# Batched matmul, 32 batches on one core: transposes of the last batches moved into their own batch, and one store split between two DMA issuers

## The chip, the cores and the metric

One core of one Trainium2 chip runs the program. The metric is device microseconds (us) of that core. The time that a run reports is about 1.7 to 2.0 us more than the span in its profile. In the profile PE is TensorE, DVE is VectorE, ACT is ScalarE, POOL is GpSimd and SP is SyncE.

## The reference

```python
def setup_inputs():
    batch, m, k, n = 32, 512, 1024, 768
    return {"x": np.random.randn(batch, m, k).astype(np.float32),
            "weight": np.random.randn(batch, k, n).astype(np.float32)}

def reference(x, weight):
    return np.matmul(x, weight).astype(np.float32)
```

Per batch the kernel reads 2 MB of x and 3 MB of weight, and writes 1.5 MB. All of it together is 168 MB read and 50 MB written.

## The kernel before

A batch's x and weight are loaded by POOL, which casts them to bf16 on the way. PE transposes x, multiplies, and ACT and DVE bring the sums from PSUM, the memory that PE writes to, to `out_sb`. The store of a batch goes out on POOL's queue one batch later. Only the first load and the two halves of the last store are issued by SP.

```python
out_view = out.rearrange("b (mi mo) n -> b mi (mo n)", mi=P)   # 12,288 bytes per partition
CHUNKED = {B - 4: (4, 4), B - 3: (4, 4), B - 2: (4, 4), B - 1: (4, 2, 2)}
AHEAD = 3
...
def load_x(b):
    xs[b] = x_pool.tile([P, MT, K], BF16, name="x_sb")
    nc.gpsimd.dma_start(out=xs[b], in_=x_view[b])
...
for b in range(B):
    if b + AHEAD < B:
        load_x(b + AHEAD)
        load_w(b + AHEAD)
    if b > 0:
        nc.gpsimd.dma_start(out=out_view[b - 1], in_=outs[b - 1])
    outs[b] = out_pool.tile([P, MT * N], F32, name="out_sb")
    if b not in CHUNKED:
        ...                                   # 28 batches, untouched by the change
        continue
    xT = ready.pop(b, None) or {mt: transpose(b, mt) for mt in range(MT)}
    pms = [banks() for _ in range(2)]
    at = 0
    for n in CHUNKED[b]:
        last = at + n == KT
        for mt in range(MT):
            if last and b + 1 < B:
                ready.setdefault(b + 1, {})[mt] = transpose(b + 1, mt)
            matmuls(pms[mt // 2], mt % 2, xT[mt], b, range(at, at + n), True)
            if last and mt % 2 == 1:
                pair = mt // 2
                evacuate(b, pair, pms[pair])
                if b == B - 1:
                    cols = slice(pair * N2, (pair + 1) * N2)
                    nc.sync.dma_start(out_view[b, :, cols], outs[b][:, cols])
        at += n
```

In the last four batches the weight comes in chunks, and the transposes of batch b+1 stand between the matmuls of batch b's last chunk. That holds for batches 29 to 31; batch 28, the first of the four, has its own transposes at its start.

## Time and profile before

| what | value |
|---|---|
| time, median of 6 runs | 516.88 us (516.58 to 517.77) |
| profiled run | 517.73 us, span 516.0 us |
| PE busy | 426.4 us (83%) |
| HBM traffic over the span | 423 GB/s |

From the page of the kernel before, the DMA rows of the 40 slices, and of the chain that ended last the first line:

```profile
DMA  8999999999999999999999999999999999999996
GB/s 255 218 218 211 215 274 275 272 272 241 255 280 273 275 254 241 276 277 274 267 240 268 274 276 272 247 252 278 275 274 256 247 267 275 276 267 239 259 390 261
...
DMA 88%; PE 9%; issue 1%; DVE 0%; ACT 0%; POOLq 0%
```

A 9 means that the sixteen DMA engines were busy for 90% of the slice or more. They are full everywhere but at the two ends, and the chain of waits is mostly transfers. So DMA bounds this kernel. Loads count at their bf16 size in this GB/s row (135.65 MB in all, where HBM saw 168 and 50 MB), so the row rises where only stores are left.

The table of stretches for the kernel before. Its columns are window, length, busy time (and count) of PE, PEld, DVE, ACT and POOL, the granted clock, the share of DMA (from packet times, so it can come out a little over 1) and GB/s:

```profile
41.00:440.00 399.00, 338.91 (x2011) 221.80 (x2049) 101.28 (x154) 60.26 (x103) 40.34 (x76) 0.94 1.02 263
490.00:505.00 15.00, 14.89 (x85) 9.49 (x86) 4.00 (x6) 2.35 (x4) 0.53 (x1) 0.89 1.03 392
505.00:516.00 11.00, 3.54 (x22) 1.95 (x20) 1.38 (x2) 2.30 (x4) 0.00 (x0) 0.90 0.56 231
```

DMA is saturated up to 505 us. Only after that is there slack, and PE is not what fills it.

The end of the timeline of the kernel before (start, length, engine, line, operation, count, and what ended the idle time before it):

```profile
489.12 0.75 PE L68 MATMUL pt<-ident,x_sb 128*128 128x128 f32 x4 [3.28 <-DMA x_sb<-in_x_dram]
...
496.67 11.86 PE L99 MATMUL pm<-w_sb,xT 128*128 128x256 bf16 x71
...
499.19 0.53 POOL L130 DMA_DIRECT2D out_dram<-out_sb  x1 [16.95 <-ACT out_sb L112]
...
507.89 1.62 SPq L159 DMA_DIRECT2D out_dram<-out_sb  x2
```

PE cannot finish batch 30 before x of batch 31 is there (489.12 us), so the store of batch 30 is issued at 499.19 us and the last two at 507.89 us and later.

The DMA queue's waits on SP, of the kernel before (who waited for whom, us in total, times, longest):

```profile
SPq L159 <- DVE out_sb L111: 507.5, 2, 506.7
SPq L186 <- DMA out_dram<-out_sb: 5.0, 3, 1.8
SPq L186 <- PEq L186: 0.9, 2, 0.5
```

L186 is the end of the program. SP waits there for the last transfers, and then for the other engines, for 0.9 us in two waits.

The trace also records when each of a transfer's sixteen completions arrived, one for each DMA engine that took part, without the engine's number. Sorted, they show how far the engines have drifted apart. These are the kernel before's, read from the completion records:

| transfer | first | last | spread |
|---|---|---|---|
| w, second load on POOL (batch 1) | 27.02 | 27.98 | 0.95 |
| x, landing at 199 us | 199.07 | 202.37 | 3.30 |
| store of batch 29 (POOL) | 502.26 | 507.45 | 5.19 |
| store of batch 30 (POOL) | 505.91 | 511.11 | 5.20 |
| batch 31, first half (SP) | 511.00 | 512.97 | 1.96 |
| batch 31, second half (SP) | 512.89 | 514.80 | 1.91 |

The engine that lands last is called the straggler below. It is 5 us behind the quickest at the end.

### The profile page before, as it was taken

What the parts mean: (1) busy time and instruction counts of PE and PEld (TensorE: products, weight loads), DVE (VectorE), ACT (ScalarE), POOL (GpSimd) and SP (SyncE); (2) the same over time, 40 slices, a digit from 0 to 9 for tenths busy, and PEclk for the clock granted to TensorE, in tenths of its full rate; (3) what the DMA queues carried; (4) which work ended last, traced back from release to release, by engine and by line L of the source; (5) the groups of instructions that cost most, each with busy time, mean ns of one, the idle gap of its engine ahead of it and who ended that gap; (6) DMA issues with size and microseconds to landing.
All of it is one profiled execution on the core that took longest, in us unless ns stands there. A gap on an engine that the chain in (4) does not pass through costs nothing.

```text
span 516.0 us, 5924 instructions
## 1 busy us (share of the span) xinstructions
PE 426.4 (83%) x2528; PEld 279.6 (54%) x2576; DVE 129.7 (25%) x196; ACT 76.3 (15%) x129; POOL 53.4 (10%) x105
## 2 busy tenths in 40 slices
PE   0999998698887879977798797987878987969794
PEld 0766665465554555654555464654545554646462
DVE  0433333133131231322313232222223132312221
ACT  0111111011111111110111011111111110101111
POOL 3011010100101001100011001010100110111000
PEclk9999999799898997998989799898989898979989
DMA  8999999999999999999999999999999999999996
GB/s 255 218 218 211 215 274 275 272 272 241 255 280 273 275 254 241 276 277 274 267 240 268 274 276 272 247 252 278 275 274 256 247 267 275 276 267 239 259 390 261
DMA packets 14714, 135.65 MB, mean 263 GB/s; under 512 B 1632, under 2 KB 1632, under 8 KB 3040
## 3 DMA queue, kind: packets, MB, share of 16 engines
q0 software_dynamic: 14256, 131.60, 98.9%
q1 hardware_dynamic: 432, 3.67, 1.9%
q8 instruction: 20, 0.33, 0.2%
q14 instruction: 6, 0.05, 0.0%
HBM read 167.77 MB, written 50.33 MB: 423 GB/s over the span
## 4 chain that ended last, share of the span: by engine, by line
DMA 88%; PE 9%; issue 1%; DVE 0%; ACT 0%; POOLq 0%
DMA x_sb<-in_x_dram 37%; DMA w_sb<-in_weight_dram 25%; DMA out_dram<-out_sb 24%; PE pm L99 7%; DMA x_first<-in_x_dram 2%; PE pt L81 1%; PE pt L68 1%; DVE out_sb L111 0%; DVE xT L70 0%; ACT out_sb L112 0%; POOLq L130 0%; POOLq L54 0%; POOLq L60 0%
## 5 line engine op out<-in xcount | busy, mean ns | idle before, releaser
L99 PE MATMUL pm<-w_sb,xT 128*128 128x256 bf16 (+1 forms) x2000 | 370.2, 340 | 60.9 <-DMA w_sb<-in_weight_dram 56.8
L99 PEld LDWEIGHTS <-xT 128*128 128x128 bf16 x2048 | 206.8, 102 | 198.3 <-issue 66.5
L70 DVE COPY xT<-pt 128x1024 bf16<-128x1024 bf16 x124 | 83.0, 689 | 245.4 <-PE pt L68 245.4
L68 PE MATMUL pt<-ident,x_sb 128*128 128x128 f32 x496 | 77.4, 290 | 8.9 <-DMA x_sb<-in_x_dram 8.6
L68 PEld LDWEIGHTS pt<-ident,x_sb 128*128 128x128 f32 x496 | 73.7, 207 | 17.2 <-issue 7.1
L110 ACT COPY out_sb<-pm 128x512 f32<-128x512 f32 x64 | 37.5, 586 | 289.6 <-PE pm L99 280.7
L111 DVE COPY out_sb<-pm 128x512 f32<-128x512 f32 x64 | 43.9, 687 | 115.5 <-PE pm L99 114.8
L112 ACT COPY out_sb<-pm 128x512 f32<-128x512 f32 x64 | 37.5, 586 | 142.5 <-PE pm L99 142.4
L54 POOL DMA_DIRECT2D x_sb<-in_x_dram x31 | 16.5, 533 | 172.8 <-DMA w_sb<-in_weight_dram 141.6
L60 POOL DMA_DIRECT2D w_sb<-in_weight_dram x37 | 19.8, 534 | 132.4 <-DMA out_dram<-out_sb 65.6
L130 POOL DMA_DIRECT2D out_dram<-out_sb x31 | 16.6, 536 | 140.8 <-DMA x_sb<-in_x_dram 62.8
L81 PE MATMUL pt<-ident,x_first 128*128 128x128 f32 x32 | 5.7, 338 | 12.4 <-DMA x_first<-in_x_dram 12.4
L81 PEld LDWEIGHTS pt<-ident,x_first 128*128 128x128 f32 x32 | 4.9, 202 | 13.0 <-issue 12.3
L82 DVE CAST xT<-pt 128x512 bf16<-128x512 f32 x8 | 5.5, 727 | 18.4 <-PE pt L81 18.3
L110 ACT ACT_TABLE_LOAD x1 | 1.3, 1283 | 0.7 <-PEq L175 0.7
masks.py:199 POOL TENSOR_SCALAR_AFFINE_SELECT ident<-ident 128x128 f32<-128x128 f32 x1 | 0.3, 288 | 0.1
masks.py:197 POOL MEMSET ident<- 128x128 f32 x1 | 0.2, 223 | 0.0
L175 POOL MEMSET const-float32-0.0<- 128x1 f32 x1 | 0.1, 99 | 0.2 <-issue 0.2
L175 POOL MEMSET const-bfloat16-1.0<- 128x1 bf16 x1 | 0.1, 102 | 0.0
L175 POOL MEMSET const-uint8-127<- 128x1 uint8 x1 | 0.1, 102 | 0.0
L175 POOL MEMSET const-float32-1.0<- 128x1 f32 x1 | 0.1, 98 | 0.0
## 6 DMA issues: line engine op xcount, KB each, us to landing
out_dram<-out_sb POOLq DMA_DIRECT2D x31, 1536.0 KB, 41.9
w_sb<-in_weight_dram POOLq DMA_DIRECT2D x28, 1536.0 KB, 43.2
x_sb<-in_x_dram POOLq DMA_DIRECT2D x31, 1024.0 KB, 39.6
w_sb<-in_weight_dram POOLq DMA_DIRECT2D x7, 768.0 KB, 32.5
x_first<-in_x_dram SPq DMA_DIRECT2D x1, 2048.0 KB, 11.5
out_dram<-out_sb SPq DMA_DIRECT2D x2, 768.0 KB, 5.3
w_sb<-in_weight_dram POOLq DMA_DIRECT2D x2, 384.0 KB, 28.7
```

What stands on the lines that cost most here:

```text
L54: nc.gpsimd.dma_start(out=xs[b], in_=x_view[b])
L60: nc.gpsimd.dma_start(out=ws[b][:, at:at + n, :], in_=w_view[b, :, at:at + n, :])
L68: nc.tensor.transpose(pt[:, j, :], pairs[:, mt, j::JT], ident)
L70: nc.vector.tensor_copy(xT.rearrange("p j m r -> p (j m r)"), pt.bitcast(BF16).rearrange("p j m -> p (j m)"))
L81: nc.tensor.transpose(pt[:, i, :], x_first[:, mt, JT * h + i::KT], ident)
L82: nc.vector.tensor_copy(xT[:, 2 * h:2 * h + 2].rearrange("p j m r -> p j r m"), pt.rearrange("p (j r) m -> p j r m", r=2),)
L99: nc.tensor.matmul(pm[bank][:, at:at + size], xT[:, ko // 2, :, ko % 2], ws[b][:, ko, off:off + size], start=(ko == 0 and not (together an ...
L110: nc.scalar.copy(o[:, 0:512], pm[0])
L111: nc.vector.tensor_copy(o[:, 512:1024], pm[1])
L112: nc.scalar.copy(o[:, 1024:N2], pm[2])
L130: nc.gpsimd.dma_start(out=out_view[b - 1], in_=outs[b - 1])
L175: nc = _bacc.Bacc("TRN2", target_bir_lowering=False, num_devices=1)
```

## The change

The change does two things. The transposes of the last four batches stand between their own matmuls (those of batches 29 to 31 come from the batch before), so PE need not hold the end of one batch until the next batch's x has landed. And the store of batch 8 is split: its first 32 partitions go as four eight-partition transfers on SP, and the other 96 as one on POOL. The likely intent of the second is to move a little load between the sixteen DMA engines.

```diff
+    FEW = {8}
...
+    def store(b):
+
+        first = 0
+        if b in FEW:
+            first = 32
+            for at in range(4):
+                nc.sync.dma_start(out_view[b, at:first:4], outs[b][at:first:4])
+        nc.gpsimd.dma_start(out=out_view[b, first:], in_=outs[b][first:])
...
-        ready = {}
...
-                nc.gpsimd.dma_start(out=out_view[b - 1], in_=outs[b - 1])
+                store(b - 1)
...
-            xT = ready.pop(b, None) or {mt: transpose(b, mt) for mt in range(MT)}
+            xT = {0: transpose(b, 0)}
...
-                    if last and b + 1 < B:
-                        ready.setdefault(b + 1, {})[mt] = transpose(b + 1, mt)
+                    if mt + 1 not in xT and mt + 1 < MT:
+                        xT[mt + 1] = transpose(b, mt + 1)
```

## The prediction

> **What bounds the kernel now.** The DMA engines. The page's DMA row is full in 39 of 40 slices; the chain of waits is 88% DMA; PE is busy 426 of 516 us. In the stretch table DMA is saturated from 2 to 505 us and falls to 0.56 after that. The trace's DMA completion records say why. Each transfer counts sixteen completions, one per engine, and these drift apart: spread 0.95 us at first, 3.3 us near 200 us, 5.2 us for the last POOL store (505.91 to 511.11 us). The steps coincide with the 20 instruction-fetch packets (16 KB, about 0.95 us each); their durations repeat with period eight, so they visit eight engines in rotation. After one rotation, at 199 us, seven engines lie within 0.6 us and nine trail by 1.2 to 3.3 us. The Trainium skill ("Runtime: NRT & Kernel Launch", Instruction fetch mechanics) describes refills in 16 KiB blocks; this trace agrees.
>
> The straggler is never idle: after 511.11 us it moves its 16 packets of the last two SP stores (0.235 us each, 3.7 us), landing at 514.80 us; the span ends 1.2 us later. Its total work is the time.
>
> **What the change does.**
>
> 1. Transposes. None is removed; twelve groups of four move from the previous batch's last chunk into their own batch. Today PE holds the last chunk of batch 30 until x of batch 31 lands (timeline: 489.12), runs to 508.5, and the store of batch 30 is issued at 499.19. Afterwards that store should be issued about 12 us earlier, PE end near 505 (estimate: w lands at 492.7, 64 matmuls at 168 ns, transposes), the last stores issue 4 us earlier. On the critical path: about nothing, since the straggler's queue is full anyway.
>
> 2. Store of batch 8. It moves 12,288-byte packets, eight per engine, each 0.457 us when stores run alone. By the skill ("DMA: Bandwidth & Descriptors", Why a DMA increments its semaphore by 16 and not by 1) an eight-partition SP transfer uses the lowest-numbered eight engines, and 96 partitions use all sixteen. So engines 0 to 7 carry 4+6=10 packets, 8 to 15 carry 6: plus or minus 0.91 us. No trace here numbers the engines; that the fetching, slow ones are 8 to 15 is a guess from the intent. If so, the straggler goes from 511.1 to 510.2, the fast half from at most 507.6 to 508.5: gain 0.9 us. If it is in 0 to 7, loss 0.9 us. Four more SP issues (0.34 us each) are off the path.
>
> **Predicted time: 516.1 us**, range 515.1 to 517.9 (8 in 10). Faster by over 2%: 0.01; within 2%: 0.98; slower by over 2%: 0.01. The 0.9 us gain has about 2 chances in 3.
>
> **What would show each step.**
> - Store: the last POOL store's completions: spread 5.2 to about 3.4 us; about 7 if the direction was wrong. Issue table: four 96 KB SP transfers, one 1152 KB POOL store.
> - Transposes: store of batch 30 issued before 490; PE's last matmul near 505; last SP stores near 504; yet the final landing unmoved by this.
> - Fetches: about 20, over eight engines.
>
> **What would make it wrong.** Fetching engines in both halves (gain then 0.2 or less); an altered fetch count or rotation; other engines for the eight-partition transfers; run-to-run spread (1.2 us, as large as the effect); or PE's tail mattering more than the straggler, worth up to 2 us more.

## The result, and the profile after

The changed kernel took 519.92 us (median of 6 runs, 519.24 to 520.54) against 516.88 us before. The ratio is 1.0056, with a 95% interval of 1.0043 to 1.0069. The change made the kernel slower by about 3 us. The predicted range ended at 517.9 us.

One caution for reading the two profiles against each other: the profiled run of before was its own slow end (517.73 us), and that of after was a little below its median (519.51 us). The two traces therefore differ by 1.8 us, not by 3.

The page of the changed kernel, the same rows:

```profile
DMA  8999999999999999999999999999999999999995
GB/s 254 218 216 212 225 263 278 272 276 244 252 292 272 276 250 230 272 276 274 270 246 256 276 275 273 261 240 273 277 274 269 243 261 271 277 270 258 238 410 216
...
DMA 81%; PE 14%; issue 1%; DVE 1%; ACT 0%; POOLq 0%
```

The table of stretches of the changed kernel:

```profile
41.00:440.00 399.00, 342.74 (x2061) 223.09 (x2059) 101.92 (x155) 60.29 (x103) 40.30 (x76) 0.94 1.02 263
490.00:505.00 15.00, 12.52 (x73) 7.91 (x72) 2.86 (x5) 0.61 (x2) 0.49 (x1) 0.89 1.03 391
505.00:516.00 11.00, 1.23 (x8) 0.58 (x6) 1.19 (x2) 1.68 (x3) 0.00 (x0) 0.73 0.56 236
```

DMA does the same work in the same stretches. PE, ACT and DVE have less left to do after 505 us, as intended.

The end of its timeline:

```profile
489.56 1.20 PE L69 MATMUL pt<-ident,x_sb 128*128 128x128 f32 x8 [0.66 <-DMA x_sb<-in_x_dram]
489.96 0.53 POOL L122 DMA_DIRECT2D out_dram<-out_sb  x1 [7.92 <-ACT out_sb L113]
...
498.27 7.96 PE L100 MATMUL pm<-w_sb,xT 128*128 128x512 bf16 x48
505.58 2.07 SPq L168 DMA_DIRECT2D out_dram<-out_sb  x2
```

The store of batch 30 is issued 9.2 us earlier and the last two 2.3 us earlier. The first part of the change did what it was meant to do.

The DMA queue's waits on SP, of the changed kernel:

```profile
SPq L168 <- DVE out_sb L112: 361.6, 2, 360.8
SPq L121 <- DVE out_sb L112: 140.5, 1, 140.5
SPq L195 <- DMA out_dram<-out_sb: 7.0, 3, 4.7
SPq L195 <- PEq L195: 2.1, 2, 1.6
```

Against before, the last line has grown from 0.9 to 2.1 us. The name PEq is what the view inferred. It is not PE: PE's last matmul ended at 506.23 us. The trace's sequencer records show that the last to arrive is GpSimd, whose own closing DRAIN instruction is still running. Here are GpSimd's DRAIN instructions at the end of the program, before and then after (count, shortest, median and longest in ns, and the first and last start in us); the longest is the first to start:

```profile
L186 POOLq DRAIN  x3: 46/102/16031, 499.2 to 515.7; - x3
```

```profile
L195 POOLq DRAIN  x3: 46/108/26759, 489.9 to 517.2; - x3
```

Its end, set beside the completion records:

| profiled run | last POOL landing | GpSimd's DRAIN ends | difference | last SP landing | DRAIN after SP landing |
|---|---|---|---|---|---|
| before | 511.11 | 515.20 | 4.09 | 514.80 | 0.41 |
| after | 512.61 | 516.70 | 4.09 | 515.14 | 1.55 |

The last data landed only 0.34 us later than before. The core ended 1.5 us later, because the DRAIN ends 4.09 us after the last landing of a POOL transfer, and that landing moved by 1.5 us. On the straggler, POOL's last store took 3.66 us before (507.45 to 511.11) and 4.79 us after (507.82 to 512.61). The two SP stores, now issued earlier, run beside it. The Trainium skill ("DMA: Bandwidth & Descriptors", Queues, rings and completion order) says that each DMA engine takes turns between the queues that have work for it, packet by packet; the longer time agrees with that.

### The profile page after: what moved, and what is told of

Its sections match the earlier page's. It is cut to its first block, busy times and chain, and to the rows that moved or that the text cites. A ratio compares the mean times of both kernels' runs of the same rounds, so it can differ in the third digit from the quotient of the medians.

```text
span 517.5 us, 5989 instructions
## 1 busy us (share of the span) xinstructions
PE 429.3 (83%) x2576; PEld 279.8 (54%) x2576; DVE 129.8 (25%) x196; ACT 76.2 (15%) x129; POOL 53.3 (10%) x105
## 2 busy tenths in 40 slices
DMA packets 14746, 135.65 MB, mean 262 GB/s; under 512 B 1664, under 2 KB 1664, under 8 KB 3072
## 4 chain that ended last, share of the span: by engine, by line
DMA 81%; PE 14%; issue 1%; DVE 1%; ACT 0%; POOLq 0%
DMA w_sb<-in_weight_dram 46%; DMA out_dram<-out_sb 25%; PE pm L100 12%; DMA x_sb<-in_x_dram 8%; DMA x_first<-in_x_dram 2%; PE pt L69 1%; PE pt L82 1%; DVE xT L71 1%; DVE out_sb L112 1%; ACT out_sb L113 0%; POOLq L61 0%; POOLq L55 0%
```

## The experiments

The theory, called theory D in the expectations: the transposes cost time because the earlier SP stores delay POOL's last store on the straggler, and GpSimd's DRAIN follows that landing; the store adds its own cost through the straggler. The main rival, called S, was that the split store is all of it. All fourteen kernels gave correct results. Each was timed against the kernel before in the same rounds, on four chips.

| run | edit to which kernel | median us | before, same rounds | ratio (95% interval) |
|---|---|---|---|---|
| e1_transposes_only | change without the store | 518.78 | 517.67 | 1.0018 (1.0005 to 1.0032) |
| e2_store_only | before with the store | 518.89 | 517.67 | 1.0020 (1.0006 to 1.0035) |
| e3_store_of_six | before, six stores split | 522.95 | 517.67 | 1.0100 (1.0082 to 1.0119) |
| e4_last_stores_on_pool | before, SP's stores on POOL | 521.43 | 517.67 | 1.0071 (1.0057 to 1.0085) |
| e5_four_partitions | before, two stores split 16 and 112 | 518.45 | 516.94 | 1.0032 (1.0020 to 1.0045) |
| e6_sp_ends | e1 with batch 30's store last on SP | 516.90 | 516.94 | 0.9999 (0.9985 to 1.0012) |
| e7_both | e5 and e6 | 517.43 | 516.94 | 1.0012 (1.0000 to 1.0025) |
| e8_after_again | the changed kernel | 520.03 | 516.94 | 1.0063 (1.0050 to 1.0076) |
| e9_store_of_20 | e2 for batch 20 | 518.17 | 516.92 | 1.0025 (1.0013 to 1.0038) |
| e10_split_even | e2, the 32 partitions as one | 519.14 | 516.92 | 1.0044 (1.0031 to 1.0057) |
| e11_after_sp_ends | change with batch 30's store last on SP | 517.73 | 516.92 | 1.0014 (1.0002 to 1.0026) |
| e12_store_on_sp | before, batch 8's store whole on SP | 518.83 | 517.11 | 1.0028 (1.0016 to 1.0040) |
| e13_split_columns | before, batch 8's store split by columns | 517.34 | 517.11 | 1.0005 (0.9993 to 1.0018) |
| e14_split_on_pool | before, batch 8's store as two on POOL | 519.45 | 517.11 | 1.0036 (1.0023 to 1.0049) |

### The two parts alone: e1 and e2

```diff
 # e1, against the changed kernel
-    FEW = {8}
+    FEW = set()
 # e2, against the kernel before
+    FEW = {8}
+    def store(b): ...                      # as in the change
-                nc.gpsimd.dma_start(out=out_view[b - 1], in_=outs[b - 1])
+                store(b - 1)
```

> The change's transposes without its store. Theory D (drain): GpSimd's closing DRAIN ends a fixed 4.09 us after the last landing of a POOL-issued transfer (515.20 after 511.11 before; 516.70 after 512.61 with the change). The early SP stores share the straggling DMA engine with the last POOL store and delay it by about 1.1 us, so this runs about 1.1 us longer than before (518.0 us), with the last SP landing unmoved (within 0.5 us) and the DRAIN again 4.09 us after the last POOL landing. Rival S (the store is all of it): no difference from before, within 0.4 us.

> The change's store of batch 8 without its transposes. Theory D with the straggler among the eight engines that got 10 packets in place of 8: about 0.9 us longer than before (517.8 us), the straggler's last POOL landing 0.9 us later. Together with the transposes that makes about 2 us of the 3.0 us measured. Rival S: the store is all of it, about 3 us longer (519.9 us). My recorded prediction: 0.9 us shorter.

The transposes alone cost 0.18% and the store alone 0.20%, about 1.0 us each. Against rival S, the transposes are not free; e1's interval begins at 0.05%, so this is narrow, and e11 below is the clearer case. The two together give 0.38%, less than the 0.56% and 0.63% of the changed kernel. That the parts make each other worse is not shown, since each of these figures is uncertain by 0.13 to 0.15%.

Both profiled runs were the fastest of their kernel (517.96 and 517.25 us), and two expectations were missed in them. In e1 the last SP landing was not unmoved but 0.95 us earlier than before (513.85 against 514.80 us). In e2 the straggler's last POOL landing was not 0.9 us later but 0.75 us earlier (510.36 against 511.11 us). So what the store alone costs is known from the times and not from its trace.

The end of e1 is as theory D has it. POOL's last store took 4.81 us on the straggler (506.50 to 511.31), the DRAIN ended 4.09 us after it at 515.40, and the last SP landing was already at 513.85. The DMA queue's waits on SP, of e1:

```profile
SPq L195 <- DMA out_dram<-out_sb: 7.3, 3, 4.9
SPq L195 <- PEq L195: 2.1, 2, 1.6
```

The last line is as in the changed kernel, without any split store. In e2's profile, with the old transposes, the DRAIN ends only 0.39 us after the last SP landing, as in the kernel before.

### Six split stores: e3

```diff
-    FEW = {8}
+    FEW = {4, 8, 12, 16, 20, 24}           # on e2
```

> Six stores split instead of one, old transposes: 12 packets of 12288 bytes move per engine, 5.5 us each way, so in the completions two halves stand 11 us apart and each step of an instruction fetch shows in which half its engine lies. If the straggler is in the half that got more: about 5.5 us longer than before (522.4 us). If it is in the other half: the other half's slowest ends it, at most 1 us longer than before.

It took 1.00% more, 5.2 us, close to the first of the two outcomes. The completions of the POOL store that begins to land at 498.4 us, us after the first one, fall into two groups of eight:

```
0.00 0.54 0.68 0.70 0.95 1.04 1.90 4.66 | 9.37 9.48 9.63 9.84 10.89 11.60 13.28 14.74
```

The late eight are those that got ten packets where the others got six. The straggler is one of them, and it is the engine that steps by about 1.1 us at the instruction fetches of 249 and 448 us, the second place in the rotation of eight. That is the place of the straggler in the kernel before too (245 and 443 us there). Fetches also step engines of the early group (3.37 to 4.63 us at 475 us). So the engines that fetch instructions lie in both groups, and the straggler lies in the group to which the change adds work. The prediction had guessed the other. The changed kernel's own trace agrees: between the loads that begin to land at 143 and 152 us, as the split store passes, the two last engines go from at most 2.22 us behind the first to 3.67 and 3.93, and one of these two (steps at 246 and 442 us) is the straggler at the end. But it need not be the same engine in every run: e8's straggler steps at the fetches of 216 and 420 us, which took 935 ns, where those of the straggler above took 893.

### All last stores on POOL: e4

```diff
-                            nc.sync.dma_start(out_view[b, :, cols], outs[b][:, cols])
+                            nc.gpsimd.dma_start(out_view[b, :, cols], outs[b][:, cols])
```

> The kernel before with the two last stores issued by POOL instead of SP. Theory D: the last POOL landing moves from 511.1 to about 514.8, the DRAIN ends 4.09 us after it, about 3.6 us longer than before (520.5 us). Rival: the DRAIN has nothing to do with POOL's landings, then within 0.7 us of before.

It took 0.71% more, 3.7 us. The last landing of all data was at 514.87 us, where it is in the kernel before (514.80), and the DRAIN ended at 519.04 us, 4.17 us later. The DMA queue's waits on SP, of e4:

```profile
SPq L186 <- PEq L186: 4.4, 2, 4.0
```

The same data landed at the same time; only the issuer of the last two stores differs. This is the plainest evidence that the closing wait belongs to POOL's transfers.

### A POOL that ends early: e6, e7 and e11

```diff
 # e6 on e1, e11 on the changed kernel, e7 on e6 with the split of e5
-            if b > 0:
+            if 0 < b < B - 1:
                 store(b - 1)
...
                 at += n
+        nc.sync.dma_start(out_view[B - 2], outs[B - 2])
```

> The change's transposes, no split store; the store of batch 30 goes out on SP after the two of batch 31, so POOL's last store is that of batch 29. Theory D: the straggler's total is as before, but POOL's last landing is near 510.5 instead of 511.3, its DRAIN ends (4.09 us later) before or with the last SP landing (near 514.5): about 1 us shorter than the transposes alone, and 0 to 0.5 us shorter than before. Rival (early stores themselves cost the microsecond, whatever POOL does): as long as the transposes alone, 1 us longer than before.

> The changed kernel again, on the chip and in the rounds of these three: 2 to 3 us longer than before, DRAIN end 4.09 us after POOL's last landing and over 1 us after the last SP landing.

> The changed kernel with the store of batch 30 moved to the end of SP, so that POOL ends early. If all of the change's loss beyond the store's 1 us comes from POOL's closing DRAIN behind the delayed last POOL store: about 1 us longer than before (518 us), 2 us shorter than the changed kernel. If not: 2 to 3 us longer than before.

e6 has the change's transposes and early SP stores like e1, but POOL's last store is that of batch 29. It runs as long as the kernel before (0.9999), so the 0.18% of e1 is not to be seen. That speaks against the rival that early stores themselves cost it, but the intervals of e1 and e6 overlap (from 1.0005, and up to 1.0012); e11 against e8, below, is clear of noise. POOL's last landing came even earlier than expected, 507.11 us, so my picture of how the two queues share the straggler was too crude there. Its DRAIN ended at 511.16 us, 3.2 us before the last SP landing. The DMA queue's waits on SP, of e6:

```profile
SPq L196 <- DMA out_dram<-out_sb: 7.0, 3, 3.6
...
SPq L196 <- PEq L196: 0.6, 2, 0.5
```

The wait is back at 0.6 us. The hoped-for gain of up to 0.5 us over before is not to be seen within the interval.

The changed kernel, run again (e8), had a ratio of 1.0063. Its DRAIN ended at 516.92 us, 2.25 us after the last SP landing (514.66). POOL's last store took 5.51 us on the straggler there (507.32 to 512.83). The DMA queue's waits on SP, of e8 and then of e11:

```profile
SPq L195 <- DMA out_dram<-out_sb: 8.7, 2, 7.1
SPq L195 <- PEq L195: 2.8, 2, 2.3
```

```profile
SPq L196 <- DMA out_dram<-out_sb: 7.8, 4, 3.6
...
SPq L196 <- PEq L196: 0.7, 2, 0.5
```

e11 is the changed kernel with POOL ending early, and its ratio is 1.0014. From 1.0056 or 1.0063 to 1.0014 is 0.42 to 0.49%, or 2.2 to 2.5 us of the change's 3 us. That is what moving POOL's last store to the end of SP gives back. The traces show 1.1 us (changed kernel) and 1.8 us (e8) of it as closing wait, against the kernel before; the last landing is also 0.4 to 0.9 us earlier in e11 (514.22 us) than in those two, and why is not shown. What is left, 0.14% or about 0.8 us, goes with the split store.

> The two preceding edits together: the sum, about 1.2 us shorter than before (0.25%), if the straggler is outside the four lowest engines; the DRAIN ends before the last SP landing.

e7 was 0.12% slower than before, not faster. The split of e5 that it contains did not pay, as the next run shows.

### What the split store costs: e5, e9, e10, e12, e13, e14

```diff
 # e5, on e2: batches 8 and 16, sixteen partitions as four four-partition transfers
-    FEW = {8}
+    FEW = {8, 16}
-            first = 32
+            first = 16
```

> The kernel before, with the stores of batches 8 and 16 split otherwise: 16 partitions as four four-partition SP transfers (four engines get 7+4=11 packets), the remaining 112 as one POOL store (the other twelve get 7 in place of 8). If the straggler is not among the four lowest engines: it loses 0.9 us over two stores, the four gain 2.7 us and stay behind it; about 0.9 us shorter than before. If it is among the four: 2.7 us longer. A theory in which each extra SP transfer costs something fixed: as long as the eight-partition stores or longer (1 to 2 us longer than before).

It cost 0.32%, 1.7 us. Neither expectation about the straggler fits: a gain was expected if it lost packets, 2.7 us of loss if it gained them. What fits is the third, 1 to 2 us of loss if each extra SP transfer costs something fixed, though e14 below loses as much with no extra SP transfer. From the completions, the straggler does not gain the 1.8 us per store that its being among the four would give (it is 3.07 us behind the first before the four-partition transfers and 2.96 us after them). But the last engine falls 1.1 us further behind soon after the shorter POOL store, near 206 us. That pointed to a cost of splitting itself.

The packets of POOL's queue show it. Nearly all of them have a few fixed durations (460 or 926 ns for 12,288 bytes, 625 ns for 8,192 bytes). Summing what the slow ones take beyond that, between 190 and 224 us, gives:

| run | POOL's part of batch 8's store | excess, us over all engines |
|---|---|---|
| before, e1, e4, e6 | 128 partitions | 0.5 to 1.1 |
| e12 | none (all on SP) | 0.4 |
| e13 | 128 partitions, three quarters of the columns | 0.5 |
| after, e2, e8, e11 | 96 partitions | 3.2 to 7.0 |
| e5, e7 | 112 partitions | 4.0 and 4.8 |
| e10 | 96 partitions | 16.0 |
| e14 | 32 and 96 partitions, both on POOL | 14.5 |
| e9 | 128 (batch 20 is split) | 0.5 |
| e3 | 96 partitions (five other batches too) | 0.4 |

```diff
 # e9, on e2
-    FEW = {8}
+    FEW = {20}
 # e10, on e2
-            for at in range(4):
-                nc.sync.dma_start(out_view[b, at:first:4], outs[b][at:first:4])
+            nc.sync.dma_start(out_view[b, :first], outs[b][:first])
```

> As the store alone, but of batch 20 instead of batch 8. All five runs that split the store of batch 8 show a burst of slow POOL packets near 204 to 208 us (4 to 9 packets, 2.4 to 4.5 us of excess in sum), and no run without it does. If the burst belongs to the shorter POOL store, it moves with it, to about 395 us, and none is left near 206. If it belongs to the time, it stays near 206. Time: 0.5 to 1.5 us longer than before either way, since the straggler gets two packets more.

> The store of batch 8 split as 32 partitions on SP and 96 on POOL, but the 32 as one transfer, so that all sixteen engines keep eight packets. If the imbalance is what the store costs (0.9 us on the straggler): no longer than before, within 0.4 us. If splitting itself costs (the burst, or another queue): about 1 us longer, as the store alone.

e9 cost 0.25%. The excess left the stretch near 206 us, and 2.4 us appeared at 384 to 400 us, as expected, so that part goes with the split and not with the time. But 4.0 us more appeared at 276 to 290 us, before the split store was issued (from 332.56 us). That part cannot come from the split, so slow packets also appear without one. e10 is the surprise. Every engine keeps eight packets, so the imbalance is gone, and it cost 0.44%, more than the uneven split. So the 1.0 us of e2, though it is the size that I had worked out for two more packets on the straggler, is not shown to be that.

Three more kernels took apart what comes with such a split:

```diff
 # e12, for batch 8: the whole store on SP
+            nc.sync.dma_start(out_view[b], outs[b])
 # e13, for batch 8: by columns, 128 partitions in each
+            nc.sync.dma_start(out_view[b, :, :N], outs[b][:, :N])
+            nc.gpsimd.dma_start(out=out_view[b, :, N:], in_=outs[b][:, N:])
 # e14, for batch 8: by partitions, both on POOL
+            nc.gpsimd.dma_start(out=out_view[b, :first], in_=outs[b][:first])
+            nc.gpsimd.dma_start(out=out_view[b, first:], in_=outs[b][first:])
```

> The whole store of batch 8 as one SP transfer of 128 partitions: it overtakes POOL's queue, nothing else. If overtaking costs: 1 us or more over before. If not: within 0.5 us of before.

> The store of batch 8 split by columns: a quarter of each of the 128 partitions on SP, three quarters on POOL; even over the engines[...]. If the partition ranges are what the even split paid for: within 0.5 us of before. If two transfers, one overtaking, cost by themselves: 1 to 2 us over before, like the even split.

> The store of batch 8 as two POOL transfers, of 32 and of 96 partitions; no SP, even over the engines. If the partition ranges cost: 1 to 2 us over before, with more excess of slow packets than before. If it is SP's overtaking: within 0.5 us of before.

e13 splits the store between SP and POOL evenly, each part over all 128 partitions, and costs nothing that the interval can tell from zero (1.0005). e14 keeps SP out of it and cuts by partitions, 32 and 96, and costs 0.36%. So two transfers in place of one, with a quarter of the store overtaking on SP, cost nothing measurable, and the cut by partitions does. The two cuts also differ in packet size, though (3,072 and 9,216 bytes in e13, 12,288 in e14), and no run tells these apart. Nor is all of the loss the split's own: in the profiles of e5, e10 and e14 the DRAIN ended 1.08, 1.32 and 1.12 us after the last SP landing, against 0.41 us before, so 0.7 to 0.9 us of it is the closing wait again. (e13 has that wait too, 1.09 us, but its last landing came 0.5 us earlier than before; e12 has 0.36 us.) e12, whole on SP, cost 0.28% with no excess near 206 us (it has 3.4 us between 150 and 170 us). A whole store that overtakes POOL's queue therefore has some price that a quarter of one (e13) does not show. Why is open.

## Why the prediction was wrong

**What bounds the kernel: right.** DMA bounds it, and the engines drift apart as described. At the end the straggler is not idle, before and after: from the landing of batch 29's store to its last it takes 7.35 and 7.32 us, and its packets alone 7.4 us (8 of 0.457 us and 16 of 0.235 us).

**The transposes: their mechanism was right, and the step to the time failed.** The store of batch 30 was issued at 489.96 us (predicted: before 490), PE ended at 506.2 us (near 505), the last SP stores began to be issued at 505.6 us (near 504), and the final landing stayed (514.80 to 515.14 us). The failing step is "On the critical path: about nothing, since the straggler's queue is full anyway", and behind it "Its total work is the time". The program does not end with the last landing. It ends when every engine has arrived, and GpSimd arrives 4.09 us after the last landing of what POOL issued. Before, that moment fell 0.41 us after the last SP landing, so it looked like part of a fixed 1.2 us tail. Moving the SP stores forward does not add work to the straggler, but it changes the order in which the straggler does it: SP's packets come in earlier and POOL's last ones later. Measured, that was 1.0 us by the transposes alone (e1 against e6: 0.19%, not clear of noise) and 2.2 to 2.5 us in company with the split store (e8 and the changed kernel against e11, clear of noise).

**The store: direction wrong.** The guess that the slow engines get less work was wrong: the straggler is in the group that gets more (e3, and the changed kernel's trace). The prediction's own test, the spread of the last POOL store, gave 6.91 us, near the 7 named for a wrong direction. But that agreement is partly luck: e1 without a split store gave 5.73 and e2 with it 4.48, since the early SP stores widen this spread and it varies from run to run. "Fetching engines in both halves" stood among the things that could upset the prediction, and they are in both. The size that was measured, 1.0 us alone and 0.8 us with POOL ending early, agrees with the 0.91 us worked out for two packets, but by e10, e13 and e14 that agreement proves nothing: an even cut by partitions costs more. What is shown is that slow packets appear near 206 us in eight of the nine runs that cut batch 8's store by partitions (all but e3, which had cut another store before it), and in none of the seven that do not. That these packets cost the time is not shown: over 41 to 500 us the same excess adds up to 16.0 us in the kernel before and 17.7 us in the changed one, and e12 lost 1.4 us with 13.7. What stays open is how much of the change's 0.8 to 1.0 us is imbalance and how much is the cut, and how packets come to be slow 10 us after it. For six stores the imbalance is plain: eight engines end 9.4 us behind the other eight.

A rule of the Trainium skill ("DMA: Bandwidth & Descriptors", Rules for kernel authors) would have been a better guide than my guess. It advises against two transfers to disjoint halves of the partitions and for one 128-partition transfer. e10 and e14, which cut at a quarter, agree with it (2.3 and 1.9 us lost), though no run here shows the reason that the page gives, that such transfers serialize, to be the cause. The page "SBUF — State Buffer" (Door 1: the DMA port swizzle) ties bandwidth to how many ports the partitions reach, and the first 32 partitions reach half of them. e13 against e10 fits that, but the excess comes after these transfers, up to 224 us, so no run here shows it to be the cause.

**The range.** The run-to-run spread was put at 1.2 us and was about that. The range was too low because a closing wait was left out, and the chance of 2 in 3 for a gain rested on a guess about which engines are slow.

**A version that beats both** was not found. e6, which keeps the change's transposes and lets SP end the program, equals the kernel before and no more, because the straggler's total is then what ends it.

## What to carry to other kernels

Ask what each engine still waits for after its last instruction: here GpSimd's closing DRAIN, 4.09 us after the last POOL landing, made the last two stores cost 3.7 us more on POOL than on SP (e4). So try the last transfers of a kernel on SP, with POOL's done some 4 us earlier. When a queue is full, issuing something earlier does not add work, but it can push back something else that the end depends on. And a split of a transfer that is even on paper must be tried on the chip: cut by columns it cost nothing measurable, cut evenly by partitions 0.36 to 0.44%, part of it closing wait.

## What the Trainium skill lacked or had wrong

- No page has the closing DRAIN on GpSimd that waits for POOL-issued transfers. In all 16 profiles here it ended 4.05 to 4.17 us after their last landing. "DMA: Bandwidth & Descriptors" counts about 2 us of fixed cost for a transfer and gives no such tail; "VectorE: DVE Perf Modes" (The DRAIN you can't avoid) tells of two kinds of DRAIN, the other being one of about 12 ns on all engines, and this one lasted 16.0 us in the kernel before, from the last POOL issue on.
- "DMA: Bandwidth & Descriptors" (Issuing engines are not separate DMA queues) says that issuing from several engines only saves the sequencer's time. It speaks of bandwidth and leaves out the end of the program. Here the issuer of the last two stores alone was worth 3.7 us (e4), through the wait just named.
- The same page does not say which engines take the instruction fetches that "Runtime: NRT & Kernel Launch" describes. The runs show 20 fetches of 16 KB, over eight engines in rotation (their durations repeat with period eight), each setting its engine back by about 1 us, and a spread of 4.5 to 6 us near the end in the kernels before and after, e1 and e2.
- No page tells of the slow packets after a store cut by partitions: 3.2 to 16.0 us over all engines between 190 and 224 us, against 0.4 to 1.1 us where POOL's part keeps all 128 partitions or there is none (one exception, e3, 0.4 us).
